# A feed-forward product by Strassen's seven products, in a two-layer decoder kernel

## The chip, the cores and the metric

The kernel runs on one core of one Trainium2 chip. The metric is the device time of one execution in microseconds (us), as the median of several runs. The engines are called PE (matrix engine, TensorE), DVE (VectorE), ACT (ScalarE), POOL (GpSimd) and SP (SyncE, which here issues transfers). Each executes its own instructions in order, and they wait for each other through semaphores.

## What is computed

x is 512 positions by 1024 features. Each of two layers adds an attention block to x and then a feed-forward block (FFN) with 2816 middle features. Cut to what matters here:

```python
def hybrid_layer(x, ...):
    ...
    x = x + merged @ w_out

    h2 = rms_norm(x, g_ffn)
    gate, up = jnp.split(h2 @ w_ffn_in, 2, axis=-1)
    return x + (jax.nn.silu(gate) * up) @ w_ffn_out

def reference(x, ...):
    for layer in range(DEPTH):
        x = hybrid_layer(x, ...)
    return rms_norm(x, norm_final)
```

## The kernel before

Features lie on the 128 partitions and positions along the free axis, so x is eight tiles `xs[m]` of 128 x 512. All products are in split precision: each operand is a high part, rounded to the type that PE takes in one pass, and a low part, the rest. `mm_tiles` issues three matmuls for each 128 x 128 weight tile: high by high (L204), low weight by high (L205) and high weight by low (L206). One weight column of 1024 inputs is 8 such tiles, so 24 matmuls of 512 columns.

Weights are streamed in a fixed order, the list `stream`. For each, SP issues a transfer of up to 512 KB into a raw buffer `wr` (two of them), ACT casts it to the high part `wh`, and DVE subtracts to get the low part `wl` (L111 and L113; POOL does some of these subtractions in the input projections alone). There are four `wh` and four `wl` buffers, and `w_get` prepares two weights ahead of the one in use.

A layer goes through these stages: the input projections with the two attentions, the output projections, the first FFN product, and the second. In the first FFN product there are 22 tiles j of 128 middle features. For each, PE computes `fg` (gate) and `fu` (up), 24 matmuls each, in a PSUM bank each; DVE multiplies both by `r`, the row factor of the norm (L623, L625), ACT applies silu (L624), POOL multiplies gate by up (L626), ACT casts to `ah` (L629), and DVE subtracts to `al` (L630). All 22 pairs `ah`, `al` are kept. In the second product each of eight outputs m is one sum over all 22 tiles, 66 matmuls, after which one DVE operation adds it to `xs[m]` (L639). Then `Norm.feed` prepares the next norm: in layer 0 the scaled high and low parts of x, `hha` on ACT and `hla` on DVE (L173, L174), and in both layers the square on ACT (L185) and its addition to `acc` (L187), on POOL for m = 1 to 5 and on DVE for 6 and 7. In layer 1 the last output, m = 7, is done in two halves of 256 columns, so that the final norm of the first half of the positions can begin before the second half is summed. `ms70` and `ms71` are the sums of that norm, by a matmul with a constant matrix.

The order on each engine is fixed when the program is built, by a scheduler that models the engines.

Of the kernel before, what the change touches and what calls it, by code (L numbers as in the profile page):

```python
# [37 lines left out]
GATES_IN_BLK = 4  # L38
FILL = (3, 3, 3, 3, 4, 4, 4, 4)
# [8 lines left out]
def trunk(ctx: ExitStack, tc, xT, par, tab, scn, msk, w_in, w_o, w_out, w_fi, w_fo, out):  # L48
# [33 lines left out]
    layer_order += [("fi", j) for j in range(2 * NH)]  # L82
    layer_order += [("fo", m, c) for m in range(8) for c in range(3)]
    stream = [(l,) + k for l in range(DEPTH) for k in layer_order]

    def w_src(k):
        l, kind, i = k[:3]
        if kind == "fo":
            c0, c1 = k[3] * 1024, min(k[3] * 1024 + 1024, HID)
            return w_fo[l, i][:, c0:c1]  # L90
        return {"in": w_in, "o": w_o, "out": w_out, "fi": w_fi}[kind][l, i]
# [23 lines left out]

    def w_prefetch():
        for _ in w_pieces(1024):
            pass

    def w_get(*key):  # L120
        while len(ready) <= W_AHEAD and state["next"] < len(stream):
            w_prefetch()
# [145 lines left out]
    for l in range(DEPTH):  # L268
# [341 lines left out]
        h = nrm.h  # L610
        with ExitStack() as fc:
            fp = fc.enter_context(tc.tile_pool(name=f"ffn{l}", bufs=1))
            act = []
            for j in range(NH):
                bg = fbank(f"fg{j}_{l}")
                mm(bg, (l, "fi", 2 * j), h)
                bu = fbank(f"fu{j}_{l}")
                mm(bu, (l, "fi", 2 * j + 1), h)
                if j == 0:
                    r = nrm.finish()  # L620
                g = fp.tile([P, S], F32, name=f"g{j}_{l}", tag="g", bufs=3)
                u = fp.tile([P, S], F32, name=f"u{j}_{l}", tag="u", bufs=3)
                nc.vector.tensor_tensor(out=g, in0=bg, in1=r, op=ALU.mult)  # L623
                silu = nc.scalar.activation(out=g, in_=g, func=AF.Silu)  # L624
                nc.vector.tensor_tensor(out=u, in0=bu, in1=r, op=ALU.mult)  # L625
                nc.gpsimd.tensor_tensor(out=u, in0=u, in1=g, op=ALU.mult)  # L626
                hi = fp.tile([P, S], F32R, name=f"ah{j}_{l}", tag="a", bufs=2 * NH)
                lo = fp.tile([P, S], F32R, name=f"al{j}_{l}", tag="a", bufs=2 * NH)
                nc.scalar.copy(out=hi, in_=u)  # L629
                nc.vector.tensor_tensor(out=lo, in0=u, in1=f32(hi), op=ALU.subtract)  # L630
                act.append((hi, lo))
            table(LNEXP, silu)
            last = l == DEPTH - 1
            nrm = Norm(C_NL if last else C_NA + 8 * (l + 1), f"a{l + 1}", split=not last)
            for m in range(7 if last else 8):
# [85 lines left out]
```

## Time and profile before

| what | value |
|---|---|
| three runs, median | 1524.53 us (1521.72 to 1525.08) |
| the profiled execution | 1526.8 us |
| its span, first instruction to last | 1525.0 us |
| PE busy | 1488.5 us, 98% |
| weight loads into PE | 1238.6 us, 81% |
| DVE busy | 853.7 us, 56% |
| ACT busy | 614.4 us, 40% |
| POOL busy | 347.4 us, 23% |

Busy time is the time in which an engine executes something; the rest it waits or has nothing to do. The granted clock in the windows is the share of full speed that PE's clock was allowed. In the groups of instructions, the first number after the bar is the busy time of the group in us, then comes the mean of one instruction in ns, then the idle time of the engine before them and what ended it.

### The profile page before, as it was taken

The page shows a single profiled execution, that of the slowest core. Times are in us where ns is not written, and L with a number is a line of the kernel's source. Part 1 is how long each engine was busy: PE and PEld are TensorE (multiplying, and loading weights), DVE is VectorE, ACT ScalarE, POOL GpSimd, SP SyncE. Part 2 cuts the span into 40 slices and gives each one's busy share as a digit, 9 for nine tenths or more (in the row PEclk, how much of TensorE's full clock was granted, in tenths as well). Part 3 has the DMA queues.
Part 4 walks back from the last instruction along what each step waited for, and adds up shares of the span by engine and source line. Part 5 has one row for each costly group of instructions (what it writes and reads, how often), then busy time and mean ns, then how long its engine had stood idle before and what let it go on. Part 6 is the DMA issues. An engine that isn't in the chain of part 4 may idle for free.

```text
span 1525.0 us, 17531 instructions
## 1 busy us (share of the span) xinstructions
PE 1488.5 (98%) x6884; PEld 1238.6 (81%) x6884; DVE 853.7 (56%) x1006; ACT 614.4 (40%) x970; POOL 347.4 (23%) x224
## 2 busy tenths in 40 slices
PE   8899999999999999999998999999999999999997
PEld 6788878888888888888877878788888888888886
DVE  5878776475545454433367787655655454544223
ACT  5655544543433232322235655446333232323221
POOL 4345652000111111101124455420021111110011
PEclk9999999999999999999999999999999999999999
DMA  6212222233233233233321223222333233323331
GB/s 208 70 56 82 78 85 88 70 110 97 97 97 97 97 97 97 90 95 95 108 96 45 91 58 97 80 74 83 97 97 97 97 97 97 97 97 91 99 101 56
DMA packets 43619, 139.59 MB, mean 92 GB/s; under 512 B 5648, under 2 KB 8080, under 8 KB 43536
## 3 DMA queue, kind: packets, MB, share of 16 engines
q1 hardware_dynamic: 42240, 137.38, 28.8%
q8 instruction: 54, 0.88, 0.2%
q10 hardware_dynamic: 1296, 1.09, 0.2%
q14 instruction: 29, 0.24, 0.0%
HBM read 132.16 MB, written 2.10 MB: 88 GB/s over the span
## 4 chain that ended last, share of the span: by engine, by line
PE 90%; DVE 5%; issue 1%; ACT 1%; DMA 1%; POOL 0%; SPq 0%; DVEq 0%; POOLq 0%; ACTq 0%
PE fu L206 5%; PE fg L205 5%; PE fg L206 5%; PE fu L205 5%; PE fg L204 5%; PE fu L204 5%; PE fo L204 5%; PE fo L205 5%; PE fo L206 5%; PE pg L204 4%; PE pg L205 4%; PE pg L206 4%; PE pd L204 3%; PE pd L205 3%; PE pd L206 3%; PE wo L204 2%
## 5 line engine op out<-in xcount | busy, mean ns | idle before, releaser
L111 ACT CAST wh<-wr 128x1024 fp32r<-128x1024 f32 (+3 forms) x251 | 258.0, 1029 | 629.7 <-PE fu L206 157.5
L113 DVE TENSOR_TENSOR wl<-wr,wh 128x1024 fp32r<-128x1024 f32 (+2 forms) x229 | 329.8, 1440 | 216.7 <-ACT wh L111 216.1
L626 POOL TENSOR_TENSOR u<-u,g 128x512 f32<-128x512 f32 x44 | 56.8, 1292 | 441.5 <-DVE u L625 394.3
L205 PE MATMUL fo<-ah,wl 128*128 128x512 f32 (+1 forms) x374 | 141.0, 377 | 0.0
L204 PE MATMUL fo<-ah,wh 128*128 128x512 f32 (+1 forms) x374 | 141.0, 377 | 0.0
L206 PE MATMUL fo<-al,wh 128*128 128x512 f32 (+1 forms) x374 | 140.8, 377 | 0.0
L204 PE MATMUL fg<-hhf,wh 128*128 128x512 f32 x352 | 137.8, 391 | 0.0
L206 PE MATMUL fu<-hlf,wh 128*128 128x512 f32 x352 | 137.0, 389 | 0.0
L205 PE MATMUL fg<-hhf,wl 128*128 128x512 f32 x352 | 137.0, 389 | 0.0
L206 PE MATMUL fg<-hlf,wh 128*128 128x512 f32 x352 | 137.0, 389 | 0.0
L204 PE MATMUL fu<-hhf,wh 128*128 128x512 f32 x352 | 137.0, 389 | 0.0
L205 PE MATMUL fu<-hhf,wl 128*128 128x512 f32 x352 | 137.0, 389 | 0.0
L625 DVE TENSOR_TENSOR u<-fu,yf 128x512 f32<-128x512 f32 x44 | 30.4, 691 | 129.2 <-PE fu L206 129.2
L204 PE MATMUL pg<-hha,wh 128*128 128x512 f32 x256 | 100.5, 392 | 0.0
L205 PE MATMUL pg<-hha,wl 128*128 128x512 f32 x256 | 100.3, 392 | 0.0
L206 PE MATMUL pg<-hla,wh 128*128 128x512 f32 x256 | 100.2, 391 | 0.0
L206 PEld LDWEIGHTS fo<-al,wh 128*128 128x128 f32 x374 | 70.4, 188 | 13.0
L205 PEld LDWEIGHTS fo<-ah,wl 128*128 128x128 f32 x374 | 70.4, 188 | 12.9
L204 PEld LDWEIGHTS fo<-ah,wh 128*128 128x128 f32 x374 | 70.4, 188 | 12.9
L113 POOL TENSOR_TENSOR wl<-wr,wh 128x1024 fp32r<-128x1024 f32 (+3 forms) x22 | 51.9, 2360 | 124.9 <-ACT wh L111 120.4
L204 PE MATMUL pd<-hha,wh 128*128 128x512 f32 x192 | 78.2, 407 | 0.5 <-ACT knd3s L341 0.5
L205 PE MATMUL pd<-hha,wl 128*128 128x512 f32 x192 | 77.7, 405 | 0.0
(270 smaller groups left out, 3093.1 us busy)
## 6 DMA issues: line engine op xcount, KB each, us to landing
wr<-in_w_fi_dram SPq DMA_DIRECT2D x88, 512.0 KB, 3.6
wr<-in_w_in_dram SPq DMA_DIRECT2D x78, 512.0 KB, 3.7
wr<-in_w_fo_dram SPq DMA_DIRECT2D x32, 512.0 KB, 3.5
wr<-in_w_o_dram SPq DMA_DIRECT2D x16, 512.0 KB, 3.6
wr<-in_w_out_dram SPq DMA_DIRECT2D x16, 512.0 KB, 3.6
wr<-in_w_fo_dram SPq DMA_DIRECT2D x16, 384.0 KB, 3.1
x<-in_xT_dram SPq DMA_DIRECT2D x8, 256.0 KB, 5.5
cs<-in_tab_dram SPq DMA_DIRECT2D x2, 512.0 KB, 5.4
```

What stands on the lines that cost most here:

```text
L111: nc.scalar.copy(out=hi[:, c], in_=raw[:, c])
L113: eng.tensor_tensor(out=lo[:, c], in0=raw[:, c], in1=f32(hi[:, c]), op=ALU.subtract)
L204: nc.tensor.matmul(dst, hi[:, c], rh, start=first and k == 0, stop=False)
L205: nc.tensor.matmul(dst, lo[:, c], rh, start=False, stop=False)
L206: nc.tensor.matmul(dst, hi[:, c], rl, start=False, stop=last and k == n - 1)
L625: nc.vector.tensor_tensor(out=u, in0=bu, in1=r, op=ALU.mult)
L626: nc.gpsimd.tensor_tensor(out=u, in0=u, in1=g, op=ALU.mult)
```

## The change

In both layers, tiles j = 3, 5, ..., 21 of the first FFN product (`FAST`, ten of 22) are computed by Strassen's scheme (Winograd's form) with seven products in place of eight. The two by two blocks are: even and odd weight tiles of the 1024 inputs (the weights are permuted on the host for it), gate and up, first and second half of the 512 positions. One product is four weight tiles by three matmuls of 256 columns. The sums of x that it needs, `s1` to `s4`, are made once per layer at the start of the FFN; the sums of the weights, `t1` to `t4`, are made for each such tile in `w_sums`, on POOL, and then split into high and low part as the others. `Fast` issues the products with copies of the running PSUM sum (`a`, `b`, `c`) between them. Its last two products (`tail`) are issued during the next ordinary tile.

In the ordinary tiles, up is no longer multiplied by `r`; `hidden` multiplies it by the gate from PSUM on DVE, and `add_x` applies `r` after the second product instead. The second product is done in four chunks of 6, 6, 6 and 4 middle tiles, each after its tiles; each chunk adds its part to x, with two DVE operations (`ft` and `x`) per m. In the last chunk, outputs 0 and 1 are begun ahead of the last tile's end, and in layer 1 outputs 4 to 7 are done in halves of 256 columns.

```diff
+CHUNKS = ((0, 6), (6, 12), (12, 18), (18, 22))
+FAST = range(3, NH, 2)
+EVEN_ODD = (0, 2, 4, 6, 1, 3, 5, 7)
...
+    def w_sums():
...
+        tf = fp.tile([P, 3, 512], F32, name=f"tf{n}", tag="tf", bufs=1)
+        tt = lambda eng, o, a, b: eng.tensor_tensor(out=o, in0=a, in1=b, op=ALU.subtract)
...
+            nc.scalar.copy(out=hi, in_=src)
+            nc.vector.tensor_tensor(out=lo, in0=src, in1=f32(hi), op=ALU.subtract)
...
+        g = parts(rg, wp, "wh", W_BUFS, [P, 2, 512])
+        tt(nc.gpsimd, tf[:, 0], ru[:, 0], rg[:, 0])
+        tt(nc.gpsimd, ru[:, 0], ru[:, 1], ru[:, 0])
+        tt(nc.gpsimd, tf[:, 1], ru[:, 1], tf[:, 0])
+        tt(nc.gpsimd, tf[:, 2], rg[:, 1], tf[:, 1])
+        t = parts(tf[:, 0:2], fp, "ta", 2, [P, 2, 512])
+        u = parts(ru, wp, "wh", W_BUFS, [P, 2, 512])
+        v = parts(tf[:, 2], fp, "tb", 1, [P, 512])
...
+            def hidden(j, g, u):
...
                 silu = nc.scalar.activation(out=g, in_=g, func=AF.Silu)
...
+                p = F("p", f"p{j}", 2)
+                (nc.vector if u.space == bass.MemoryType.PSUM else nc.gpsimd).tensor_tensor(
+                    out=p, in0=u, in1=g, op=ALU.mult)
...
+                def __init__(self, j):
...
+                    prod(self.r0, self.w["b11"], A["a11"], True)
+                    self.a = self.snap("a")
...
+                def middle(self):
...
+                    prod(self.r2, w["t1"], A["s1"], True)
+                    prod(self.r0, w["t2"], A["s2"])
+                    b = self.snap("b")
+                    prod(r1, w["b21"], A["a12"], True)
...
+                    prod(self.r0, w["t3"], A["s3"])
+                    c = self.snap("c")
...
+                def tail(self):
...
+                    prod(self.r0, w["t4"], A["a22"])
+                    nc.vector.tensor_tensor(out=self.g[:, H:], in0=self.r0, in1=r[:, H:], op=ALU.mult)
+                    prod(self.r2, w["b22"], A["s4"])
...
+            def add_x(b, m, ts=slice(0, S)):
+                x = xs[m][:, ts]
+                t = F("p", f"ft{m}", 2)[:, ts]
+                nc.vector.tensor_tensor(out=t, in0=b, in1=r[:, ts], op=ALU.mult)
+                nc.vector.tensor_tensor(out=x, in0=t, in1=x, op=ALU.add)
...
+            for m in range(4 if last else 8):
+                if m < 2:
+                    _, b, (hi, lo) = head[m]
+                    mm_tiles(b, hi, lo, aa[n:], False, True, n)
+                else:
+                    b = fbank(f"fo{m}{c}_{l}")
+                    mm(b, (l, "fo", m, c), aa)
+                add_x(b, m)
                 nrm.feed(m)
...
+                ws = [w_get(l, "fo", m, c) for m in range(4, 8)]
                 for t in range(2):
                     ts = slice(t * H, t * H + H)
+                    for m, (hi, lo) in zip(range(4, 8), ws):
+                        b = fbank(f"fo{m}{t}")
+                        mm_tiles(b[:, :H], hi, lo, [(u[:, ts], v[:, ts]) for u, v in aa], True, True)
+                        x = xs[m][:, ts]
+                        add_x(b[:, :H], m, ts)
+                        sq = F("p", f"sq{m}{t}", 2)[:, :H]
+                        nc.scalar.activation(out=sq, in_=x, func=AF.Square)
```

The change moves instructions on every engine. On DVE, near the end of layer 1, the additions to x stood three weight subtractions apart (`fo0_1` is output 0 of layer 1; `wl230` is the low part of the 230th weight of the stream):

```order
L639 TENSOR_TENSOR x0_93<-fo0_1_10563,x0_93 128x512
L113 TENSOR_TENSOR wl230_10684<-wr230_10682,wh230_10683 128x1024
L113 TENSOR_TENSOR wl231_10714<-wr231_10712,wh231_10713 128x1024
L113 TENSOR_TENSOR wl232_10744<-wr232_10742,wh232_10743 128x768
L639 TENSOR_TENSOR x1_94<-fo1_1_10651,x1_94 128x512
L113 TENSOR_TENSOR wl233_10774<-wr233_10772,wh233_10773 128x1024
L113 TENSOR_TENSOR wl234_10804<-wr234_10802,wh234_10803 128x1024
L113 TENSOR_TENSOR wl235_10834<-wr235_10832,wh235_10833 128x768
L639 TENSOR_TENSOR x2_95<-fo2_1_10741,x2_95 128x512
```

In the changed kernel the same place, behind the last tile of middle features, reads so (`fo03_1` is the part of output 0 from chunk 3, `fo40` the first half of output 4):

```order
L756 TENSOR_TENSOR ft0_1_12710<-fo03_1_12675,yf1_9884 128x512
L756 TENSOR_TENSOR ft1_1_12718<-fo13_1_12682,yf1_9884 128x512
L130 TENSOR_TENSOR wl240_12728<-wr240_12726,wh240_12727 128x512
L757 TENSOR_TENSOR x0_93<-ft0_1_12710,x0_93 128x512
L130 TENSOR_TENSOR wl241_12754<-wr241_12752,wh241_12753 128x512
L757 TENSOR_TENSOR x1_94<-ft1_1_12718,x1_94 128x512
L756 TENSOR_TENSOR ft2_1_12744<-fo23_1_12725,yf1_9884 128x512
L756 TENSOR_TENSOR ft3_1_12770<-fo33_1_12751,yf1_9884 128x512
L757 TENSOR_TENSOR x2_95<-ft2_1_12744,x2_95 128x512
L757 TENSOR_TENSOR x3_96<-ft3_1_12770,x3_96 128x512
L130 TENSOR_TENSOR wl242_12779<-wr242_12777,wh242_12778 128x512
L756 TENSOR_TENSOR ft4_1_12802<-fo40_12789,yf1_9884 128x256
```

Two operations for each m, and one subtraction of half the width, have taken the place of one operation and three subtractions; `wl242` stands behind seven operations that belong to outputs 0 to 3.

On ACT, around the end of the first FFN product of layer 1, the load of the other function table stood behind the last silu, with casts of weights around both:

```order
L111 CAST wh226_10565<-wr226_10564 128x768
L624 ACTIVATE g21_1_10551<-g21_1_10551 128x512
L213 ACT_TABLE_LOAD
L111 CAST wh227_10595<-wr227_10594 128x1024
L629 CAST ah21_1_10557<-u21_1_10552 128x512
L111 CAST wh228_10625<-wr228_10624 128x1024
L111 CAST wh229_10653<-wr229_10652 128x768
```

Now the copy of a running sum and the last silu, which wait for tile 21's last products, and the table load stand ahead of the cast of `wh239`, the weight of `fo33`:

```order
L727 COPY c21_1_12637<-fa21_1_12566 128x256
L696 ACTIVATE g21_1_12621<-g21_1_12621 128x512
L268 ACT_TABLE_LOAD
L128 CAST wh239_12684<-wr239_12683 128x512
L701 CAST ah21_1_12669<-p21_1_12667 128x512
L128 CAST wh240_12727<-wr240_12726 128x512
L128 CAST wh241_12753<-wr241_12752 128x512
L237 ACTIVATE acca2_12674<-x0_93 128x512
L804 ACTIVATE x0_93<-x0_93,pt_70 128x512
```

Casts of weights for outputs 4 and 5 (`wh240`, `wh241`) stand behind the cast of tile 21's result.

On PE, the sum of the final norm's first half, `ms70`, stands directly behind the first half of output 7, as it did before, but three more outputs' second halves now follow it:

```order
L259 MATMUL fo70_12849<-ah21_1_12669,wh243_12784 128x256
L260 MATMUL fo70_12849<-ah21_1_12669,wl243_12785 128x256
L261 MATMUL fo70_12849<-al21_1_12670,wh243_12784 128x256
L822 MATMUL ms70_12867<-acca2_12674,ones_d_77 128x256
L259 MATMUL fo41_12894<-ah18_1_12110,wh240_12727 128x256
L260 MATMUL fo41_12894<-ah18_1_12110,wl240_12728 128x256
L261 MATMUL fo41_12894<-al18_1_12111,wh240_12727 128x256
```

`acca2` is the sum of squares of outputs 0 to 6. Before, it was completed during the first half of output 7; now outputs 4 to 6 are added to it in halves, while the first halves of outputs 5 to 7 run.

## Rows read from the trace of the kernel before

**Rows 1.** The page: span, busy time of PE, and the chain that ended last.
```profile
span 1525.0 us, 17531 instructions
...
PE 1488.5 (98%) x6884; PEld 1238.6 (81%) x6884; DVE 853.7 (56%) x1006; ACT 614.4 (40%) x970; POOL 347.4 (23%) x224
...
PE 90%; DVE 5%; issue 1%; ACT 1%; DMA 1%; POOL 0%; SPq 0%; DVEq 0%; POOLq 0%; ACTq 0%
```

**Rows 2.** Windows of both FFN products, the boundary and layer 1's attention.
```profile
core 0: us, PE busy (x) PEld busy (x) DVE busy (x) ACT busy (x) POOL busy (x), PEclk, DMA share, GB/s
400.00:641.00 241.00, 241.00 (x1063) 199.24 (x1062) 117.56 (x114) 75.80 (x93) 27.13 (x21) 1.00 0.31 97
641.00:760.00 119.00, 119.00 (x526) 98.55 (x526) 40.28 (x40) 32.40 (x39) 12.93 (x7) 1.00 0.32 94
740.00:795.00 55.00, 54.99 (x248) 45.05 (x247) 26.56 (x27) 18.98 (x24) 12.24 (x9) 1.00 0.34 106
760.00:880.00 120.00, 113.16 (x559) 93.65 (x558) 86.36 (x84) 61.59 (x110) 49.34 (x26) 0.99 0.25 79
880.00:1000.00 120.00, 115.50 (x570) 97.93 (x571) 89.02 (x130) 62.62 (x130) 60.18 (x39) 0.96 0.26 79
1391.00:1514.00 123.00, 122.92 (x605) 104.22 (x604) 36.30 (x40) 31.96 (x40) 13.00 (x9) 1.00 0.27 80
```

**Rows 3.** Timeline of PE around 1496.6, from whole to halved columns: start, duration.
```profile
1496.22 0.39 PE L205 MATMUL fo<-ah,wl 128*128 128x512 f32 x1
1496.45 0.39 PE L206 MATMUL fo<-al,wh 128*128 128x512 f32 x1
1496.67 0.28 PE L204 MATMUL fo<-ah,wh 128*128 128x256 f32 x1
1496.79 0.28 PE L205 MATMUL fo<-ah,wl 128*128 128x256 f32 x1
```

**Rows 4.** Timeline of DVE and POOL around two weight subtractions.
```profile
500.91 1.29 POOL L626 TENSOR_TENSOR u<-u,g 128x512 f32<-128x512 f32 x1 [9.59 <-DVE u L625]
...
501.18 2.10 DVE L113 TENSOR_TENSOR wl<-wr,wh 128x1024 fp32r<-128x1024 f32 x1 [0.44 <-ACT wh L111]
...
506.62 1.23 DVE L113 TENSOR_TENSOR wl<-wr,wh 128x1024 fp32r<-128x1024 f32 x1 [0.44 <-ACT wh L111]
```

**Rows 5.** Groups of POOL by line and shape.
```profile
L626 POOL TENSOR_TENSOR u<-u,g 128x512 f32<-128x512 f32 x44 | 56.8, 1292 | 441.5 <-DVE u L625 394.3 <-ACT g L624 47.2
...
L187 POOL TENSOR_TENSOR acca<-acca,sqa 128x512 f32<-128x512 f32 x15 | 25.7, 1717 | 170.6 <-ACT sqa L185 170.6
```

**Rows 6.** Groups of DVE by line and shape.
```profile
L630 DVE TENSOR_TENSOR al<-u,ah 128x512 fp32r<-128x512 f32 x44 | 29.8, 678 | 0.0
...
L174 DVE SCALAR_TENSOR_TENSOR hlf<-x,pt,hhf 128x512 fp32r<-128x512 f32 x16 | 11.9, 746 | 0.0
...
L639 DVE TENSOR_TENSOR x<-fo,x 128x512 f32<-128x512 f32 x15 | 10.4, 692 | 32.9 <-PE fo L206 32.9
```

**Rows 7.** Timeline of the tail, from the last fo matmul.
```profile
1513.21 0.28 PE L206 MATMUL fo<-al,wh 128*128 128x256 f32 x1
...
1514.28 0.41 DVE L654 TENSOR_TENSOR x<-fo,x 128x256 f32<-128x256 f32 x1
...
1518.37 3.35 DVE L664 TENSOR_TENSOR x<-x,yz 128x256 f32<-128x256 f32 x5
```

**Rows 8.** Groups of ACT by line and shape.
```profile
L111 ACT CAST wh<-wr 128x1024 fp32r<-128x1024 f32 x230 | 242.0, 1053 | 561.2 <-PE fu L206 157.5 <-PE fg L206 113.8 <-PE fo L206 89.5
L624 ACT ACTIVATE g<-g 128x512 f32<-128x512 f32 x44 | 27.6, 626 | 3.3 <-DVE g L623 3.3
L629 ACT CAST ah<-u 128x512 fp32r<-128x512 f32 x44 | 27.4, 623 | 45.5 <-POOL u L626 45.5
...
L624 ACT ACT_TABLE_LOAD x2 | 2.6, 1283 | 0.0
```

**Rows 9.** The page's list of transfers: KB each, median us to landing.
```profile
wr<-in_w_fi_dram SPq DMA_DIRECT2D x88, 512.0 KB, 3.6
```

More of the change, by code (lines that the diff above doesn't have):

```diff
@@ L81, in trunk @@
     layer_order += [("o", m) for m in range(8)] + [("out", m) for m in range(8)]
[L82 to L83 removed]
+    FFN = []
+    for c, (j0, j1) in enumerate(CHUNKS):
+        FFN.append(("j", j0))
+        if c:
+            FFN.append(("c", c - 1))
+        FFN += [("j", j) for j in range(j0 + 1, j1)]
+    FFN.append(("c", len(CHUNKS) - 1))
+    for kind, i in FFN:
+        if kind == "c":
+            layer_order += [("fo", m, i) for m in range(8)]
+        elif i not in FAST:
+            layer_order += [("fi", 2 * i), ("fi", 2 * i + 1)]
+        else:
+            layer_order.append(("fs", i))
     stream = [(l,) + k for l in range(DEPTH) for k in layer_order]
@@ L120, in w_get @@
     def w_get(*key):
-        while len(ready) <= W_AHEAD and state["next"] < len(stream):
+        while state["next"] < len(stream):
+            ahead = sum(2 if r[0][1] == "fs" else 1 for r in ready[1:])
+            if ready and ahead >= W_AHEAD:
+                break
             w_prefetch()
@@ L610, in trunk @@
         h = nrm.h
+        nrm_f = nrm
         with ExitStack() as fc:
[L612 to L623, printed above, removed]
-                silu = nc.scalar.activation(out=g, in_=g, func=AF.Silu)
[L625 to L631, printed above, removed]
@@ new lines, in add_x @@
+            def add_x(b, m, ts=slice(0, S)):
[3 more added lines that the diff above has]
+                nc.vector.tensor_tensor(out=x, in0=t, in1=x, op=ALU.add)
+            late = []
+            for kind, i in FFN:
+                if kind == "j" and i not in FAST:
+                    bg = fbank(f"fg{i}_{l}")
+                    mm(bg, (l, "fi", 2 * i), hq)
+                    for o in late:
+                        silu = o.tail()
+                    late = []
+                    bu = fbank(f"fu{i}_{l}")
+                    mm(bu, (l, "fi", 2 * i + 1), hq)
+                    if i == 0:
+                        r = nrm_f.finish()
+                    g = F("g", f"g{i}", 2)
+                    nc.vector.tensor_tensor(out=g, in0=bg, in1=r, op=ALU.mult)
+                    silu = hidden(i, g, bu)
+                elif kind == "j":
+                    f = Fast(i)
+                    f.middle()
+                    late = [f]
+                elif i < len(CHUNKS) - 1:
+                    for m in range(8):
+                        b = fbank(f"fo{m}{i}_{l}")
+                        mm(b, (l, "fo", m, i), [act[j] for j in range(*CHUNKS[i])])
+                        add_x(b, m)
@@ L632, in trunk @@
+            for o in late:
+                silu = o.tail()
             table(LNEXP, silu)
-            last = l == DEPTH - 1
+            c = len(CHUNKS) - 1
+            aa = [act[j] for j in range(*CHUNKS[c])]
             nrm = Norm(C_NL if last else C_NA + 8 * (l + 1), f"a{l + 1}", split=not last)
-            for m in range(7 if last else 8):
-                b = fbank(f"fo{m}_{l}")
-                for c in range(3):
-                    mm(b, (l, "fo", m, c), act[8 * c:8 * c + 8], c == 0, c == 2)
-                nc.vector.tensor_tensor(out=xs[m], in0=b, in1=xs[m], op=ALU.add)
+            head = [(m, fbank(f"fo{m}{c}_{l}"), w_get(l, "fo", m, c)) for m in range(2)]
```

105 lines of the change are left out of this document (88 added, 17 removed).

## The prediction

> **What bounds the kernel now.** I read the head of the page first. The matrix engine PE is busy 98% of the span, and 90% of the chain that ended last is PE's own work [rows 1]; the other engines stand at 56% and below. The windows then show where this is strictly so: in both FFN products PE is busy for the whole stretch at a granted clock of 1.00, and at the boundary between the layers it does not pause either; only the attention of layer 1 has holes, 6.8 and 4.5 us in two stretches of 120 us [rows 2]. So in the stages that the change touches, matmul time is the time, and everything on DVE, ACT and POOL is hidden. Two questions follow: how much matmul time goes away, and whether the other engines still fit under what is left, above all where a stage ends and nothing can run ahead.
>
> **What is removed from PE.** In the timeline the 512-column matmuls of the second product start 0.227 us apart and the 256-column ones 0.120 apart, more than half of it [rows 3]. An ordinary tile of middle features is 48 matmuls of 512 columns: 48 x 0.227 = 10.88 us. A Strassen tile is 7 products x 4 weight tiles x 3 = 84 matmuls of 256: 84 x 0.120 = 10.08. Seven eighths of the arithmetic thus saves 0.80 us or 7%, not 12.5%. Ten tiles in each of two layers: -16.0. In the last chunk of layer 1, 4 x 12 matmuls are halved where before 66 of one m were; a halved one costs 2 x 0.120 - 0.227 = 0.013 more, so -0.24. PE's saving is **-16.2 us**, and it is firm unless the new products run at another pace than the old halved ones.
>
> **What is added on the other engines, in the middle of a stage.** A pair (one Strassen tile with the ordinary tile after it) lasts 10.08 + 10.88 = 20.96 us on PE. DVE and POOL together get: 3.5 weight subtractions of 1024 for the Strassen tile and 2 for the ordinary one, about 1.23 us each when alone [rows 4], four sums of 512 on POOL at 1.29 and one product [rows 5], and some 4 x 0.42 + 4 x 0.69 of small operations [rows 6, 7]; 15 to 18 us if none of it overlapped, under 20.96. ACT gets 5.5 casts of 1.05, two silu and two casts of 0.62 [rows 8] and three copies of 256: some 9.5. Nothing is full. What can still wait is the order. The tightest place is the copy of the first product from PSUM, which the t2 product must not overtake: it stands on ACT behind the casts of the two weights that follow, and the second of these waits for the end of the ordinary tile (T = 21.0 from the pair's start). 21.0 + 1.05 + 0.62 + 0.4 plus hand-overs is 23.3; t2 comes after 36 matmuls of 256, at 21.0 + 4.3 = 25.3. Two us to spare: I cost the pairs, the sums of x at the start of the stage (issued behind one ordinary tile and needed three tiles later) and the first three chunks, whose eight results come 4.1 us apart, at **nothing**. Cover gone, a pair would pay what the fourth rival says.
>
> **What is added where a layer ends.** Before, each of the 8 outputs m of the second product took 66 matmuls, 15 us, and DVE had one add for it. Now the last chunk has 12 per m, 2.72 us, and each m needs two operations of 0.69 (L756 and L757 in the order shown), its weight subtraction (0.68 as the 512-wide ones), and in layer 0 also hla (0.75 as hlf) [rows 6]: 2.8 us of DVE for 2.7 of PE. Further, fo03, fo13, fo23 and fo33 wait together for the last Strassen tile and end within 0.7 us of each other. I follow layer 1 by hand, T = 0 at tile 21's first product.
> (1) PE goes through tile 21 and what it may do of fo03 to fo23 until 16.4. fo33 needs wh239, which ACT casts behind silu and the table load, 1.28 [rows 8]: 15.5 + 0.63 + 1.28 + 0.62 = 18.1, then the subtraction: PE stands **2.4 us**. (Before, a whole 15-us product covered that load.)
> (2) fo03 to fo33 end from 23.1 to 23.75. DVE then does ft0, ft1, wl240: 25.1. fo40 stands **1.4**.
> (3) x0, wl241 until 26.5, in time for fo50, which ends at 27.9. Then x1, ft2, ft3, x2, x3 ahead of wl242: 5 x 0.69 + 0.68 = 4.1, 30.6. fo60 stands **2.7**.
> (4) fo70 ends at 33.4. The first matmul of the final norm stands in PE's order ahead of all second halves, and waits for acc of m 6: ten operations of 0.42 to 0.46 on DVE from 31.7, to 35.7: **2.3**.
> (5) The tail. Before, 11.8 us lie between the start of the last fo matmul and the end of the span [rows 7], and the first half's multiplications had been done under the second half's matmuls. Now the five of them on DVE (3.35) come after the last x, the second half's behind them, and ACT issues four output transfers before the Exp of the second half. By the same durations: 13.6, **+1.9**.
> Sum of layer 1: 10.7. In layer 0, (1) is the same, 2.4; (2) is 1.4; wl120 comes 0.8 late; the first input projection of layer 1 waits for wl122 behind x3, wl121, ft4, hla12, ft5, hla13, x4, x5: 1.4. Sum 6.0. Together **16.7**, as if DVE never had to share.
>
> **DVE and POOL hold each other up.** A wl of 1024 takes 1.23 us alone and 2.10 when a POOL operation began 0.27 before it [rows 4]: it ended 1.08 after POOL's, as if it had waited for POOL's end. The squares of m 1 to 5 in layer 0 and of 1 to 3 in layer 1 are added on POOL, 1.29 alone, 1.72 on average [rows 5], and fall just into the stretches in which DVE now sets the pace. If each stops DVE fully: 5 x 1.29 less what falls into DVE's own waits, some 3.5 us in layer 0 and 3.9 in layer 1: 24.1 in place of 16.7. The Trainium skill, page "SBUF — State Buffer", on the port pair that DVE and GpSimd share, says that it is an exclusive lock held for a whole instruction, by a DVE operation with two SBUF inputs too; by that the sum would be the upper one, 24.1, less the ft operations, which read PSUM. By that rule, the row agrees.
> The row shows the full wait, but for one pair of operations; in these stretches some of POOL's additions will fall into DVE's own waits for PE. I take two thirds of the way, 16.7 + 4.9 = 21.6.
>
> **Sum.** -16.2 + 21.6 = +5.4; bounds -16.2 + 16.7 = +0.5 and -16.2 + 24.1 = +7.9. On the profiled execution, 1526.8 with its span of 1525.0, this is 1532.2. That execution lies 2.3 above the median of the runs, 1524.5, so against the median: **1529.9**. Not in it: layer 1's attention is issued in another order in places, and its 11.3 us of holes [rows 2] can shrink or grow; I allow 5 either way. A hole also costs clock: the stretch with 6.8 us of holes was granted 0.99, the next 0.96 [rows 2]; against 21.6 us of new holes that is 1 us or so, within this allowance. Transfers stay hidden: one of 512 KB lands in 3.6 us [rows 9].
>
> **Rivals.**
> First, *faster*: the layer ends cost little. The one mechanism is DVE's order there: if the results of the last chunk reach DVE one after the other rather than together (fo33 a tile earlier), steps (2) to (4) and layer 0's share shrink to the table load and the tail, 2 x 2.4 + 1.9 = 6.7, net -9.5, 1515. It decides as soon as the ends cost less than 16.2. For it: the durations that I add are means that include waits. Against it: PE's order puts the last matmuls of four outputs behind tile 21, and DVE was doing wl of 1024 there with 15 us per m before.
> Part of that case, with 3 in 100: Strassen's products come closer together than the old halved ones did. At half the spacing of a 512-column matmul, 0.1135, a tile would take 9.53, save 1.35, and all twenty 27, so 1529.9 - 11 = 1519; but no two of the halved ones in the trace start closer than 0.12 [rows 3]. Near that lies the Trainium skill, page "TensorE: Matmul & The Clock Gate", section "Back-to-back issue gap": 262 cycles for 256 columns and 518 for 512 at 2.4 GHz, an estimate of 109 and 216 ns, by which a tile would save 1.2 us and all of them 24. The trace agrees with neither figure.
> Second, *no change*: the ends and the gain cancel: the lower bound of the sum, with the attention a little better, 1522 to 1527.
> Third, the forecast, 1527.5 to 1537.
> Fourth, *much slower*: the ring of weights sets the pace inside the pairs. Two raw buffers, a cast on ACT in order, a subtraction on DVE, a transfer: from the release of a weight by PE, 1.05 (cast) + 1.23 (subtraction) + 3.6 (transfer) + 1.05 + 0.62 + 0.4 (copy) is some 8 us, against 5.7 in which the next copy is wanted if the released slot is that of the Strassen tile's last product. That would be +2.7 at each of 10 to 12 transitions: +27 to +32, less where they overlap with the ends, 1545 to 1560. Against it: the slot that comes free first is the ordinary tile's, earlier in the pair, and by it there are 2 us to spare. It decides when a hand-over or a lock costs more than those.
>
> **How the numbers follow.** Forecast 0.42; much slower 0.14; no change 0.19; faster 0.25. Within 0.2%, 3 us, no measurement of this kernel can tell a change. Slower is 0.42 + 0.14 = 0.56. The likeliest case alone runs from 1527.5 to 1537. For 8 in 10 I take all of it and of "no change", the upper half of "faster" (1517 up) and the near part of "much slower" (to 1543).
>
> **What would show it.** Right: 256-column products of a Strassen tile 0.12 apart, PE without a pause between tiles 3 and 20; PE idle 2 to 3 us ahead of fo33 in both layers with ACT as the releaser; idle ahead of fo40 and fo60 released by DVE wl; idle at the final norm released by DVE; 13 to 15 us after the last fo matmul; about 17 to 24 us of new PE idle in all. Wrong: pauses at each Strassen tile's t2 (the fourth rival), or layer ends with under 10 us of idle (the first), or another spacing of the matmuls.

## The result: 13 us slower

The changed kernel takes 1537.93 us in the median (1536.11 to 1539.11) against 1524.8 for the kernel before; the ratio is 1.0089, with a 95% interval from 1.0073 to 1.0104. The forecast was slower, 1529.9 in a range from 1517 to 1543. The profiled execution took 1538.4 us, its span is 1536.5.

The head of the page of the changed kernel (busy time by engine, then the chain that ended last):

```profile
span 1536.5 us, 19620 instructions
...
PE 1484.0 (97%) x7586; PEld 1264.0 (82%) x7586; DVE 977.4 (64%) x1258; ACT 685.6 (45%) x1116; POOL 441.9 (29%) x306
...
PE 82%; DVE 10%; ACT 3%; DMA 2%; issue 2%; SPq 1%; POOL 1%; DVEq 0%; ACTq 0%; POOLq 0%
```

Against [rows 1], PE's share of the chain has gone from 90 to 82%, and DVE, ACT and transfers have taken its place. PE is busy only 4.5 us less than before, though 16.2 us of matmul work are gone: busy time counts a slow matmul as busy. Where the time is spent shows when the span is cut into stages. The table is worked out from the starts of PE's instructions in the timelines, in us: FFN 0 runs from the first `fg` matmul of layer 0 to the first norm sum of layer 1, so it holds the end of layer 0 and the first projections of layer 1; attention 1 goes from there to the first output projection; FFN 1 from the first `fg` of layer 1 to the end of the last `fo` matmul; the tail is the rest of the span. The rows below the second are the experiments of the next section.

| kernel | to FFN 0 | FFN 0 | attention 1 | output projections 1 | FFN 1 | tail | span |
|---|---|---|---|---|---|---|---|
| before | 401.05 | 376.25 | 287.37 | 87.04 | 361.78 | 11.51 | 1525.0 |
| changed | 400.62 | 378.72 | 289.41 | 87.04 | 366.35 | 14.36 | 1536.5 |
| late table load | 401.31 | 379.55 | 290.89 | 87.04 | 368.76 | 14.35 | 1541.9 |
| pause filled | 397.81 | 376.71 | 283.75 | 87.04 | 367.33 | 14.36 | 1527.0 |
| last chunk of 6 | 400.85 | 375.62 | 291.28 | 87.04 | 365.87 | 14.14 | 1534.8 |
| no Strassen tile | 400.85 | 377.53 | 286.61 | 87.04 | 361.12 | 16.75 | 1529.9 |
| tile 21 ordinary | 400.15 | 371.66 | 285.16 | 87.56 | 359.25 | 14.82 | 1518.6 |
| same, one output halved | 397.89 | 371.68 | 284.51 | 87.56 | 358.33 | 14.03 | 1514.0 |
| no POOL at the ends | 399.08 | 375.67 | 292.47 | 87.04 | 365.65 | 14.19 | 1534.1 |
| same, late table load | 400.37 | 375.56 | 291.92 | 87.04 | 367.91 | 14.20 | 1537.0 |
| Strassen 1 to 19 | 399.90 | 374.02 | 290.07 | 87.04 | 364.23 | 14.74 | 1530.0 |
| tile 21 ordinary, last chunk of 6 | 400.22 | 373.23 | 284.20 | 87.09 | 357.94 | 14.12 | 1516.8 |
| tile 21 ordinary in layer 0 only | 400.33 | 371.66 | 285.13 | 87.07 | 364.91 | 14.10 | 1523.2 |

Each FFN stage should have become 8.1 us shorter and became 2.5 and 4.6 us longer. So the end of layer 0 costs 10.6 us, that of layer 1 12.7, its tail 2.9, and attention 1 2.0; with 0.4 less at the start this is 27.7 - 16.2 = 11.5, the difference of the two spans.

The gain itself is there. PE in the timeline of the changed kernel at its first Strassen product (start, duration); the spacing is 0.12 as in [rows 3]:

```profile
444.91 0.28 PE L712 MATMUL fa<-sh,whh 128*128 128x256 f32 x1
445.03 0.28 PE L712 MATMUL fa<-sh,whl 128*128 128x256 f32 x1
```

PE's waits in the FFN stage of layer 0, then in that of layer 1 and the tail (what waited, for what, us in total, times, longest); in layer 0 all of them lie in the last 45 us of the stage, in layer 1 in the last 30:

```profile
PE p L259 <- ACT wh L128: 2.8, 1, 2.8
PE fo L259 <- ACT wh L128: 1.8, 1, 1.8
PE fo L260 <- DVE wl L130: 1.0, 3, 0.5
...
PE fo L259 <- ACT wh L128: 3.3, 3, 1.8
PE ms L822 <- DVE acca L819: 2.6, 2, 1.8
PE fo L260 <- DVE wl L130: 1.0, 3, 0.5
PE ms L823 <- ACT sq L816: 0.4, 1, 0.4
```

These are the places that the prediction named: `fo33` on ACT's cast, `fo43` or `fo40` and `fo60` on weights, the first projection of layer 1, the final norm. But they add up to 12.9 us only, because of two things that the list does not count. A matmul's modelled end lies up to 0.2 us behind the start of the next, so that each pause counts short. And behind some of the pauses the matmuls themselves are slow. PE around `fo33` in layer 1 (the bracket is the idle time before an instruction, and what ended it):

```profile
1493.11 0.28 PE L712 MATMUL fc<-sl,whh 128*128 128x256 f32 x1
1495.15 0.50 PE L259 MATMUL fo<-ah,wh 128*128 128x512 f32 x1 [1.76 <-ACT wh L128]
1495.88 0.79 PE L260 MATMUL fo<-ah,wl 128*128 128x512 f32 x1 [0.23 <-DVE wl L130]
1496.47 0.63 PE L261 MATMUL fo<-al,wh 128*128 128x512 f32 x1
1496.90 0.63 PE L259 MATMUL fo<-ah,wh 128*128 128x512 f32 x1
```

After the pause the 512-column matmuls start 0.43 us apart, not 0.227. The windows give the reason (busy time of each engine, the granted clock before the last two columns):

```profile
741.50:744.50 3.00, 3.00 (x8) 2.32 (x7) 0.00 (x0) 0.00 (x0) 0.00 (x0) 0.50 0.26 78
1480.00:1493.00 13.00, 13.00 (x85) 11.56 (x84) 2.86 (x5) 1.83 (x4) 0.73 (x1) 1.00 0.16 43
...
1496.00:1499.00 3.00, 3.00 (x7) 2.36 (x8) 0.64 (x1) 0.00 (x0) 0.00 (x0) 0.50 0.30 87
1509.00:1512.50 3.50, 3.35 (x16) 3.35 (x17) 3.36 (x7) 2.49 (x5) 2.53 (x2) 0.55 0.00 0
```

PE is fully busy from 1480 to 1493 at full clock, stands for 2.4 us, and then runs at 0.50, the 1.2 GHz level, for about 3 us; so it does in layer 0 at 741.5, and again behind the pauses at `fo60` in layer 1. At half speed 3 us cost 1.5: 1.5 + 1.5 + 3.5 x 0.45 = 4.6 us that no wait shows. Not every pause is followed by it. The longest of them, at the first projection of layer 1 (3.2 us between two starts, 759.56 and 762.75), has full clock behind it:

```profile
763.00:779.00 16.00, 15.98 (x70) 12.86 (x70) 12.12 (x11) 6.86 (x11) 8.31 (x7) 1.00 0.47 164
```

### The profile page after: what moved, and what is told of

The parts are those of the page before. It is cut to its first block, busy times and chain, and to the rows that moved or that the text cites. A ratio compares the mean times of both kernels' runs of the same rounds, so it can differ in the third digit from the quotient of the medians.

```text
span 1536.5 us, 19620 instructions
## 1 busy us (share of the span) xinstructions
PE 1484.0 (97%) x7586; PEld 1264.0 (82%) x7586; DVE 977.4 (64%) x1258; ACT 685.6 (45%) x1116; POOL 441.9 (29%) x306
## 4 chain that ended last, share of the span: by engine, by line
PE 82%; DVE 10%; ACT 3%; DMA 2%; issue 2%; SPq 1%; POOL 1%; DVEq 0%; ACTq 0%; POOLq 0%
PE fa L712 8%; PE fo L260 5%; PE fo L259 5%; PE fo L261 5%; PE fc L712 4%; PE pg L259 3%; PE pg L260 3%; PE pg L261 3%; PE fg L260 3%; PE fu L260 3%; PE fg L259 3%; PE fu L261 3%; PE fg L261 3%; PE fu L259 3%; PE pd L259 2%
## 5 line engine op out<-in xcount | busy, mean ns | idle before, releaser
L128 ACT CAST wh<-wr 128x1024 fp32r<-128x1024 f32 (+3 forms) x227 | 217.7, 964 | 317.7 <-PE fo L261 50.6
L130 DVE TENSOR_TENSOR wl<-wr,wh 128x1024 fp32r<-128x1024 f32 (+2 forms) x205 | 255.1, 1248 | 68.3 <-ACT wh L128 67.7
L698 POOL TENSOR_TENSOR p<-u,g 128x512 f32<-128x512 f32 x20 | 25.8, 1289 | 194.8 <-DVE u L750 194.8
L756 DVE TENSOR_TENSOR ft<-fo,yf 128x512 f32<-128x512 f32 (+1 forms) x68 | 43.7, 656 | 59.3 <-PE fo L261 59.0
L261 PEld LDWEIGHTS fo<-al,wh 128*128 128x128 f32 x368 | 70.6, 192 | 12.9
L145 POOL TENSOR_TENSOR tf<-ru,rg 128x512 f32<-128x512 f32 x20 | 31.8, 1590 | 169.0 <-DMA ru<-in_w_fi_dram 168.9
L242 POOL TENSOR_TENSOR accf<-accf,sqf 128x512 f32<-128x512 f32 x10 | 18.5, 1846 | 206.8 <-ACT sqf L240 206.8
L261 PE MATMUL pd<-hla,wh 128*128 128x512 f32 x192 | 77.9, 406 | 0.0
L260 PE MATMUL fg<-hhf,wl 128*128 128x512 f32 x192 | 75.6, 394 | 0.0
L259 PE MATMUL fg<-hhf,wh 128*128 128x512 f32 x192 | 75.5, 393 | 0.0
L260 PE MATMUL fu<-hhf,wl 128*128 128x512 f32 x192 | 75.1, 391 | 0.0
```

The source lines that it names most:

```text
L128: nc.scalar.copy(out=hi[:, c], in_=raw[:, c])
L130: eng.tensor_tensor(out=lo[:, c], in0=raw[:, c], in1=f32(hi[:, c]), op=ALU.subtract)
L145: tt = lambda eng, o, a, b: eng.tensor_tensor(out=o, in0=a, in1=b, op=ALU.subtract)
L242: eng.tensor_tensor(out=self.acc, in0=self.acc, in1=sq, op=ALU.add)
L259: nc.tensor.matmul(dst, hi[:, c], rh, start=first and k == 0, stop=False)
L260: nc.tensor.matmul(dst, lo[:, c], rh, start=False, stop=False)
```

## The experiments

**The table load late, and the pause filled.** The first theory was the prediction's own: chains on ACT and DVE, and a price for each pause in clock behind it. The first kernel takes the cause that the trace names for the pause at `fo33` away; the second leaves the pause's length and gives PE something to do in it.

```diff
-            table(LNEXP, silu)
...
+                state["sq"] = nc.scalar.activation(out=sq, in_=x, func=AF.Square)
...
+            table(LNEXP, state["sq"])
```

> The changed kernel with one instruction moved: the load of the other function table on ACT (1.28 us) stands behind the squares of the last chunk instead of ahead of the cast of wh239, in both layers. My theory (the layer ends are chains on ACT and DVE, and each pause of PE there costs a second time by a lower clock behind it): the pause of 2.4 us ahead of fo33 shrinks to about 1.1, twice -1.3; if the shorter pause leaves the clock at 1.00, the 2.0 and 2.1 us of half-speed matmuls behind it go too: 1538 - 2.6 - 4.1 = 1531; with the clock falling all the same 1535. Rival (ACT is not what ends last there; the results al of tile 21 are): no change, 1538 +- 1. Rival (the load is only moved to a place that waits as much, the norm): 1538 to 1540.

Measured 1539.2 us, ratio 1.0095 (1.0079 to 1.0111): nothing gained. The instructions of PE stand in the same order as in the changed kernel. DVE, ACT and POOL just ahead of `fo33` in layer 1, first in the changed kernel:

```profile
1494.48 0.62 ACT L128 CAST wh<-wr 128x512 fp32r<-128x512 f32 x1
...
1495.13 0.69 DVE L130 TENSOR_TENSOR wl<-wr,wh 128x512 fp32r<-128x512 f32 x1 [1.28 <-ACT wh L128]
```

and then with the late load:

```profile
1496.97 0.62 ACT L128 CAST wh<-wr 128x512 fp32r<-128x512 f32 x1 [0.26 <-PE fc L712]
...
1497.54 1.27 POOL L698 TENSOR_TENSOR p<-u,g 128x512 f32<-128x512 f32 x1 [11.36 <-DVE u L750]
...
1497.62 1.73 DVE L130 TENSOR_TENSOR wl<-wr,wh 128x512 fp32r<-128x512 f32 x1 [0.23 <-ACT wh L128]
```

The last matmul of the last Strassen product starts at 1493.11 and 1496.65. Counted from there the cast now begins 1.05 us earlier; what it waits for now is that product itself (`<-PE fc`). But the subtraction behind it now meets POOL's product of tile 21 and takes 1.73 us in place of 0.69: it ends at about the same distance, 2.7 us, as before the edit. PE's first `fo33` matmul starts earlier, the second not; the two pauses add up to 2.41 us against 2.42. The third expectation, that the load would be in the way elsewhere, is not needed for this. The table load was what ended last; right behind it stood a POOL operation that would have done the same.

```diff
+                    end = prod(self.r2, w["b22"], A["s4"])
+                    if self.j == NH - 1:
+                        with tc.issue_after(end.ins):
+                            for i in range(20):
+                                nc.tensor.matmul(self.full[:, H:], A["a11"][0][0][:, :P], A["a22"][0][0], start=True, stop=True, skip_group_check=True)
```

> The changed kernel with 20 more matmuls of 256 columns (2.4 us at 0.12) behind tile 21's last product in each layer, whose results nobody reads: they fill the pause ahead of fo33 and shorten nothing. My theory (the clock falls because PE paused): clock 1.00 in the 4 us behind it, matmuls there 0.227 apart and not 0.427, so 2.0 and 2.1 us less: 1538 - 4 = 1534. Rival (the clock falls for another reason, as the dense stretch of 256-column products before it): no change or, with the added work, 1538 to 1539.

Measured 1530.27 us, ratio 1.0034 (1.0023 to 1.0046): 40 matmuls more, and the kernel is faster. The windows behind the filled pause, in layer 0 and layer 1, and a later one:

```profile
737.00:740.00 3.00, 3.00 (x16) 2.41 (x15) 1.25 (x2) 0.62 (x1) 0.01 (x1) 1.00 0.32 87
1485.00:1488.00 3.00, 3.00 (x15) 2.38 (x14) 0.74 (x2) 0.16 (x1) 0.00 (x0) 1.00 0.30 87
1503.50:1508.50 5.00, 5.00 (x23) 4.82 (x23) 1.11 (x3) 1.41 (x4) 0.00 (x0) 0.50 0.02 3
```

The clock behind the filled pause is 1.00 in both layers, as the theory had it. By itself this does not show that the pause makes the clock fall, because the same pause, left empty, is not always followed by a fall. In the kernel without POOL at the ends, described below, PE stands as long ahead of `fo33` in layer 0, and the clock behind it is 1.00:

```profile
736.10 0.28 PE L712 MATMUL fc<-sl,whh 128*128 128x256 f32 x1
738.13 1.02 PE L259 MATMUL fo<-ah,wh 128*128 128x512 f32 x2 [1.76 <-ACT wh L128]
...
738.20:745.00 6.80, 6.49 (x24) 4.38 (x25) 3.36 (x6) 1.54 (x3) 0.00 (x0) 1.00 0.14 39
```

It is the same in layer 1 of the kernel with tile 21 ordinary in layer 0 only (1.00 from 1483.3 to 1490). So of five such pauses, idle for 1.76 us and ended by ACT's cast, three were followed by 0.50 and two by 1.00; what decides between them is open. That filling them keeps the clock up is better seen in the mean granted clock of whole executions: 0.986 to 0.989 in the six of the filled kernel, 0.981 to 0.986 in the four of the changed one.

FFN 0 became 2.0 us shorter. FFN 1 became 1.0 us longer: the pauses that follow in it are 2.7 us at `fo60` and 3.1 at the norm, and from 1503.5 the clock is 0.50 for 5 us. The rest of the difference of the spans, 2.8 us ahead of the FFN, where the instructions are the same, and 5.7 in attention 1, is mostly clock as well: 0.99 here against 0.98 ahead of the FFN, and in attention 1, first in the changed kernel and then here:

```profile
779.34:1068.75 289.41, 276.13 (x1355) 232.38 (x1354) 206.07 (x260) 154.09 (x291) 109.90 (x65) 0.97 0.24 77
...
774.52:1058.27 283.75, 272.61 (x1356) 228.20 (x1354) 203.92 (x260) 153.74 (x291) 109.20 (x65) 0.99 0.24 78
```

Why it fell less there, far from the edit, is not known.

**Which part of the change makes the ends expensive.** Two more kernels of the same kind: a larger last chunk, and no Strassen tile at all.

```diff
-CHUNKS = ((0, 6), (6, 12), (12, 18), (18, 22))
+CHUNKS = ((0, 4), (4, 10), (10, 16), (16, 22))
```

> The changed kernel with chunks of 4, 6, 6 and 6 tiles instead of 6, 6, 6 and 4: the small chunk comes first, and each output of the last one takes 18 matmuls, 4.08 us, for 2.8 us of DVE. My theory (in the last chunk DVE, with POOL's additions in its way, and ACT cannot follow PE at 2.72 us an output): the pauses ahead of fo63, of the first input projection of layer 1 and of fo60 mostly go, with the clock lost behind them; the ones ahead of fo33 and fo43 stay: 1538 - 5 to - 10, so 1528 to 1533. Rival (the first four outputs end together whatever the size of the chunk, and that alone makes the loss): 1536 to 1538.

Measured 1535.15, ratio 1.0064 (1.0049 to 1.0078), a gain of 2.8 against 5 to 10 expected. The pause at layer 1's first projection is gone, but the small chunk now stands in front, and behind it the next Strassen tile waits. PE at that place in layer 0:

```profile
478.47 0.28 PE L712 MATMUL fa<-hlf,whh 128*128 128x256 f32 x1
479.93 0.39 PE L712 MATMUL fc<-sh,tah 128*128 128x256 f32 x1 [1.19 <-ACT tah L150]
```

`tah` is the sum of the next tile's weights: a weight of a 4-tile output is used up in 2.72 us, and the streaming that was hidden in the pairs seems not to be hidden after eight of those. The three pauses there, at `tah`, at the first copy and at the next weight, come to 2.4 us.

```diff
-FAST = range(3, NH, 2)
+FAST = ()
```

> The changed kernel with no Strassen tile: all 22 are ordinary, the four chunks, add_x and the halves at the end stay (the unused sums of x at the start too). PE's matmul time goes back by 16.2. My theory (the chunks, above all the last one, cost what eats the gain; nothing is lost in the pairs): slower than before, by what the last chunk costs without the late products of tile 21: between 12 and 26 us over 1524.8, so 1537 to 1551, and 1544 as the middle. Rival (the loss belongs to the Strassen tiles: their late products at the end): 1525 to 1531.

Measured 1532.05, ratio 1.0043 (1.003 to 1.0056). This fell between the two and against my theory. With 8.1 us more of matmuls in each stage than the changed kernel, FFN 0 is 1.2 us shorter than there, and FFN 1 5.2 us shorter. The same last chunk, at the same 2.72 us an output and with `ft`, `x` and `wl` for each output on DVE as there, costs 1.3 us at the end of layer 0 and nothing visible in layer 1 before the norm. What costs is 16.75 - 11.51 = 5.2 us of tail. PE's waits of that run in FFN 0, and in FFN 1 with the tail:

```profile
PE p L259 <- ACT wh L128: 0.7, 1, 0.7
...
PE ms L822 <- DVE acca L819: 3.0, 1, 3.0
```

So the load of the chunk on DVE was not the cause by itself. What differs is what stands ahead of the chunk. The next kernels leave the chunks alone and make tile 21 ordinary, so that 3, 5, ..., 19 are Strassen tiles:

```diff
-FAST = range(3, NH, 2)
+FAST = range(3, NH - 2, 2)
```

> The changed kernel with Strassen tiles 3, 5, ..., 19 only, nine of 22: tile 21, the last of the first product, is an ordinary one. PE's matmul time rises by 0.8 a layer. Theory after the run with no Strassen tile (there the layer ends cost 1.3 us in layer 0 and nothing in layer 1, with the same last chunk): the loss is not in the chunk but in having a Strassen tile right ahead of it, whose last two products have nothing behind them and whose result comes late, so that four outputs end together. Then layer 0's FFN takes 377.5 - 7.2 = 370.3 and layer 1's 361.1 - 7.2 = 353.9, and the whole 1532 - 14.4 = 1517 to 1518, faster than before by 7. Rival (it is the load on DVE in the last chunk, and the run without Strassen tiles only hid it by its lighter middle): 1538 + 1.6, at best 1535.

Measured **1516.61 us, ratio 0.9946 (0.9932 to 0.996)**, 0.4 us under the expectation: faster than before the change, and 21 us faster than the changed kernel, with one Strassen tile less in each layer. PE's waits in the FFN stage of layer 0 and in that of layer 1 with the tail are now:

```profile
PE p L261 <- DVE hla L229: 1.2, 1, 1.2
...
PE ms L822 <- DVE acca L819: 4.1, 2, 2.6
PE ms L823 <- ACT sq L816: 0.4, 1, 0.4
```

No `fo` matmul waits any more. FFN 0 and FFN 1 are each 7.1 us shorter than in the changed kernel though they hold 0.8 us more matmul work, so a Strassen tile right ahead of the last chunk cost 7.9 us in each layer, ten times what it saves. Attention 1 is 4.3 us shorter, at a clock of 0.98 for 0.97.

To see the two ends apart, tile 21 was made ordinary in layer 0 alone:

```diff
-FAST = range(3, NH, 2)
+FAST = (range(3, NH - 2, 2), range(3, NH, 2))
...
-                if kind == "j" and i not in FAST:
+                if kind == "j" and i not in FAST[l]:
```

> Tile 21 ordinary in layer 0, Strassen in layer 1: the two ends apart. Theory (each end loses by itself what its late Strassen tile costs): layer 0's FFN as in the run with tile 21 ordinary in both layers (371.7 us from its first matmul to the first norm sum of layer 1), layer 1's as in the changed kernel (366.4): about 1524 to 1526. Layer 1's attention took 289 to 292 us in the runs with a Strassen tile at the end of layer 0, once 284, and 285 to 287 in those without. If that is a consequence of layer 0's end, it is 285 here; if it is chance, or comes from the program's other parts, 284 to 292.

Measured 1525.72, ratio 1.0011 (1.0003 to 1.002). FFN 0 is 371.66 as with tile 21 ordinary in both layers, FFN 1 364.91, near the changed kernel; the 1.4 us between them are the clock, which here stayed at 1.00 behind the pause at `fo33`. Each end loses by itself. Attention 1 took 285.13.

**POOL beside DVE.** Does it matter that POOL holds DVE up at the ends? There DVE's `x` took 1.42 us for 0.68 and `wl` 1.78 for 0.68 in the changed kernel, each beside one of POOL's additions of squares, and each ended 0.55 us after it:

```profile
751.26 1.29 POOL L242 TENSOR_TENSOR acca<-acca,sqa 128x512 f32<-128x512 f32 x1 [11.47 <-ACT sqa L240]
...
754.46 1.66 POOL L242 TENSOR_TENSOR acca<-acca,sqa 128x512 f32<-128x512 f32 x1 [1.90 <-ACT sqa L240]
...
751.68 1.42 DVE L757 TENSOR_TENSOR x<-ft,x 128x512 f32<-128x512 f32 x1
...
754.29 0.68 DVE L757 TENSOR_TENSOR x<-ft,x 128x512 f32<-128x512 f32 x1
754.89 1.78 DVE L130 TENSOR_TENSOR wl<-wr,wh 128x512 fp32r<-128x512 f32 x1
```

```diff
-                eng = nc.vector if k >= 6 else nc.gpsimd
+                eng = nc.vector if k >= 6 or self.name in ("a1", "a2") else nc.gpsimd
...
-                (nc.vector if u.space == bass.MemoryType.PSUM else nc.gpsimd).tensor_tensor(
+                (nc.vector if u.space == bass.MemoryType.PSUM or j == NH - 1 else nc.gpsimd).tensor_tensor(
```

> The changed kernel with no POOL operation at the layer ends: the squares of all outputs in the last chunk are added on DVE, and so is the last product of tile 21 formed there. DVE gets 6 operations of 0.69 more in layer 0 and 4 in layer 1. Theory (a POOL operation holds a DVE operation up for its whole 1.27 us: in the profile of the changed kernel x took 1.42 and 2.13 for 0.69 and 1.28, wl 1.78 for 0.68): the waits ahead of fo63, the first input projection and fo60 shrink by 1 to 2 each although DVE has more to do: 1538 - 2 to - 5. Rival (DVE's own work is what is late): 1538 + 2 to + 4.

and, with the table load moved as in the first experiment on top of that edit,

> As the run without POOL at the layer ends, with the table load behind the squares as well. In the run with the late load alone the wait ahead of fo33 stayed 2.4: ACT's cast came 1.05 earlier, but the subtraction on DVE behind it took 1.73 for 0.69, beside POOL's last product of 1.27. Theory (that subtraction was held up by POOL): now the wait ahead of fo33 falls to 1.9 (u, the product on DVE 0.69, wl 0.69 behind each other), and if the clock stays, 2 us a layer more; against the run without POOL -1 to -5. Rival (something else holds it): the wait stays 2.4 and the time that of the run without POOL.

Measured 1538.5 (1.0088, 1.0074 to 1.0103) and 1537.31 (1.0084, 1.007 to 1.0099). Both intervals hold the changed kernel's ratio, and the first kernel came out neither 2 to 5 us faster nor 2 to 4 slower. FFN 0 is 3.1 us shorter in both, more than half of it because the clock stayed at 1.00; attention 1 takes 3.1 and 2.5 longer, FFN 1 is 0.7 shorter and 1.6 longer. In the second kernel the pause ahead of `fo33` is 1.85 us, as worked out, so it was POOL that kept it at 2.41; the total does not show it. What is gained at the end of layer 0 goes again in attention 1: in the first kernel PE stands there for 16.3 us in place of 13.3, 2.0 of them in one wait for DVE (5.3 for 3.3), and its clock is 0.96 for 0.97. That DVE is late there because it now does POOL's additions itself is likely and not shown.

**Three tries at the rest.**

```diff
-FAST = range(3, NH, 2)
+FAST = range(1, NH - 2, 2)
```

> Ten Strassen tiles a layer as in the changed kernel, but 1, 3, ..., 19 instead of 3, 5, ..., 21: the last tile is ordinary, and the first Strassen tile comes right behind tile 0. Theory (a Strassen tile costs where nothing follows it, not by itself): twice 0.8 us less than the run with tiles 3 to 19, 1516.6 - 1.6 = 1515, if the sums of x are ready in time for tile 1. Rival (they are not: they need some 8 scalings on ACT and 12 sums on DVE at the start of the stage): PE pauses 1 to 6 us a layer there, 1518 to 1527.

Measured 1531.75, ratio 1.0054 (1.0039 to 1.0068): the rival's mechanism, and almost 5 us beyond its range. Besides the sums of x that come late at tile 1, copies and weights do, which neither expectation had. PE's waits in FFN 0 say so:

```profile
PE p L259 <- ACT wh L128: 1.5, 1, 1.5
PE fa L712 <- ACT c L727: 0.8, 1, 0.8
PE fc L712 <- DVE tal L151: 0.6, 1, 0.6
PE fc L712 <- DVE sl L688: 0.6, 1, 0.6
```

Against the kernel with tiles 3 to 19, FFN 0 is 2.4 us longer, about what these waits are worth; FFN 1 is 5.0 longer and attention 1 4.9. In FFN 1 the pauses around the first Strassen tile come to 3.4 us, and the last 34 us of the stage run at 0.90 in place of 0.95, 1.7 more. In attention 1 PE stands 1.9 us longer and its clock is 0.97 for 0.98; why is open.

With tile 21 ordinary, only output 7 was then done in halves, as before the change:

```diff
-            for m in range(4 if last else 8):
+            for m in range(7 if last else 8):
...
-                ws = [w_get(l, "fo", m, c) for m in range(4, 8)]
+                ws = [w_get(l, "fo", m, c) for m in range(7, 8)]
```

> As the run with tile 21 ordinary, and only output 7 of layer 1 is done in halves, as before the change, instead of outputs 4 to 7. One theory (the halves of four outputs cost: DVE has 16 operations more of 0.42 at the end, the first half's multiplications cannot lie under the second half's matmuls, and the tail is 16.7 instead of 11.5): 3 to 5 us less than that run, 1513. Rival (the halves help, since the norm's first half begins earlier): 1 to 4 us more, 1519 to 1521.

Measured 1518.67, ratio 0.9959 (0.9946 to 0.9972), not to be told from 0.9946, and between the two expectations. The halves of four outputs show neither a gain nor a cost.

The last of the three has tile 21 ordinary and the chunks of 4, 6, 6 and 6 shown above.

> Strassen tiles 3 to 19, tile 21 ordinary, and chunks of 4, 6, 6 and 6. Theory (what is left at the ends, 1.9 us of pauses at the start of layer 1 and 2.6 us ahead of the final norm, is DVE and POOL that cannot follow 2.72 us an output): at 4.08 us an output these waits go, 1516.6 - 3 to - 4 = 1513. Rival (in the changed kernel a last chunk of 6 gave 2.8, and that was only its tile 21's share): 1516 to 1517, no change against the run with tile 21 ordinary.

Measured 1518.65, ratio 0.9966 (0.9953 to 0.9978): no gain either. The wait at the start of layer 1 is gone and that for the norm's sum fell from 4.1 to 0.8; PE's waits in FFN 0 and in FFN 1 with the tail show that others have come around the small first chunk:

```profile
PE fa L712 <- ACT a L727: 1.1, 2, 0.8
PE fc L712 <- ACT tah L150: 1.1, 1, 1.1
PE fg L260 <- DVE wl L130: 0.4, 1, 0.4
...
PE fa L712 <- ACT a L727: 1.6, 1, 1.6
PE ms L822 <- DVE acca L819: 0.8, 1, 0.8
```

## Why the prediction was right, and what was off

The sign was right, and the time lies in the stated range. The size was not right: +13.1 us against +5.4, above the sum's own upper bound of +7.9 and just above the 1537 of the likeliest case. The range held it only because it reached into "much slower", the case of pauses inside the pairs, which did not happen; that is luck.

**The saving of 16.2** was right to the step: 0.120 us between Strassen's matmuls, and no pause between tiles 3 and 20 in layer 0. The trace does not agree with the 109 and 216 ns that the prediction worked out from the Trainium skill, page "TensorE: Matmul & The Clock Gate", section "Back-to-back issue gap": 0.120 and 0.227 us here as before. The pairs and the first three chunks cost nothing, as worked out, but the margin of 2 us is thin: behind a chunk of 4 in place of 6, PE pauses 2.4 us. In the prediction's arithmetic, 48 x 0.227 is 10.90 and not 10.88, the ten operations of step (4) are 4.2 to 4.6 us and not 4.0 if nothing overlaps, and the fourth rival's 8 us against 5.7 leave 2.3 and not 2.7; nothing here hangs on them.

**The waits at the ends** were at the places named, and five of six within a half us (distance between two starts, less that of an undisturbed matmul): `fo33` 2.42 in both layers (2.4), `fo60` 2.7 (2.7), the norm 1.9 (2.3), `fo63` 0.7 (0.8), `fo43` and `fo40` 1.1 and 1.3 (1.4). The first projection of layer 1 waited 3.0 us where 1.4 was worked out: `wl121`, held up by POOL to 1.78 us, released its raw buffer late, and the transfer and the cast of the next weight came behind it, a chain that the prediction had left out. Without the clock the ends cost 10.6 + 12.7 + 2.9 - 4.6 = 21.6 us, as forecast; that they agree to the decimal is luck, since the upper share for POOL had been a choice, and other parts made up for it: the pauses above come to 15.5 and the tail to 2.9, and the other 3.2 were not located. The tail, +2.9, was costed at +1.9.

**The step that was mis-sized is the clock's**: "against 21.6 us of new holes that is 1 us or so". It was worked out from the mean over stretches of 120 us of attention, 0.99 and 0.96. These rows already spoke against a price by the us of hole: the stretch with more of them had the higher clock. Behind three of the pauses, and not behind the longest, the clock is 0.50 for about 3 us, and the sum is 4.6 us. In the run with the filled pauses two of these three falls are missing and the kernel is 7.7 us faster; that a pause brings a fall each time is not so. Attention 1 added 2.0, within the 5 allowed for it.

**The reason given for the waits** was half wrong. The prediction said that the first four outputs wait together for tile 21 and that DVE, at 2.8 us an output for 2.7 of PE, cannot follow. The first half fits what the runs show; the second is not enough by itself: without Strassen tiles the same chunk at the same rate paused PE 0.9 us in layer 0. There, counting 12 matmuls an output, DVE begins on the first output at 746.01, and PE has the rest of the third and the whole fourth to do until 749.89. In the changed kernel DVE begins at 746.21, the last matmuls of the first four outputs stand together there, and PE comes to the fifth at 746.93, 0.7 us behind DVE and not 3.9.

**Not settled**: attention 1 took 284 to 292 us in runs whose instructions in it are the same or nearly so. It was 289 to 292 in the changed kernel and in four of the five experiments that end layer 0 on a Strassen tile, and 284 in the fifth; it was 284 to 287 in the kernel before and in five experiments that do not, and 290 in a sixth. In every one the granted clock of the stage goes with it: 0.99 in the two of 284 and 285 us with the pause filled and with one output halved, 0.98 in the others up to 287, 0.97 at 289 and 290, and 0.96 from 291 up. So most of the difference is time at half speed. The end of layer 0 may bear on how often the clock falls in the attention behind it, but these are single executions, and which wait would carry it over was not tried.

## What to carry to other kernels

Ask of a cheaper scheme where its results come out late, and see that something ordinary follows it: here one unit of ten, the last in its stage, cost ten times what it saved, and making it ordinary turned a loss of 0.9% into a gain of 0.5%. When the engine that bounds a kernel is full, a new pause of it can cost twice, the wait and slow matmuls behind it; look for the second in windows of a few us behind the pause, since a list of waits does not hold it, and do not take it as certain, since the same pause cost it in three places and not in two. Before removing what ended a wait last, look at what ends just before it: the table load hid a POOL operation that kept the wait as long.

## What the hardware showed that I had not expected

With twenty matmuls of no use in a pause of 2.4 us in each layer the granted clock behind it was 1.00 where it had been 0.50 for 3 us, FFN 0 became 2.0 us shorter, and the kernel 7.7. Yet the same pause without them had 1.00 behind it in two other runs, and the changed kernel's longest pause, 3.2 us, did as well: whether a pause of this size costs clock differed from place to place and from run to run. And a DVE subtraction of 512 columns, 0.69 us alone, took 1.73 when a POOL product of 1.27 had begun 0.08 us before it: it ended 0.54 us after POOL's, as if it had waited out the whole operation. That is what the Trainium skill says, page "SBUF — State Buffer", section "Who interferes with whom", of DVE operations with two SBUF inputs beside GpSimd; this row agrees.
